# Transposing the attention weights of a prompt: from TensorE to 32x32 blocks on VectorE and a trip through DRAM

## The chip, the cores and the metric

The kernel runs on one core of a Trainium2 chip. A core has engines with an instruction list each, run in order: TensorE (PE in the profile; its weight loads are PEld), VectorE (DVE), ScalarE (ACT), GpSimd (POOL) and SyncE (SP). They meet by semaphores and through the on-chip memories SBUF and PSUM. DMAs to and from DRAM are issued here from the lists of SyncE and ScalarE; the profile shows these issues as SPq and ACTq, and the packets of the two as queues q1 (SyncE) and q10 (ScalarE). The metric is the time of one execution on the device in microseconds, and of several executions the median.

## The reference

One layer of a hybrid decoder. The prompt (1024 tokens, width 1024) and 8x4 sample tokens go through one input projection. Its columns feed an RWKV-7 time mixing (8 heads of 64) and a dilated attention: 3 groups of window and dilation, 4 heads of 128 each. Gates merge the two branches, an output projection and a LayerNorm follow. The change lies in the attention of the prompt:

```python
A_GROUPS = ((128, 1), (512, 4), (2048, 16))          # window, dilation
s = jnp.einsum('bdnqhe,bdnkhe->bdnhqk', qb, kc) * (1.0 / math.sqrt(E))
s = jnp.where(valid, s, NEG)
m = jnp.max(s, -1, keepdims=True)
p = jnp.exp(s - m)
l = jnp.sum(p, -1)
o = jnp.einsum('bdnhqk,bdnkhe->bdnqhe', p, vc)        # / l, then merged over the groups by softmax of the log sums
```

Tokens of one residue class modulo the dilation form a sequence, and each block of 128 queries sees its own block of keys and the one before. For 1024 tokens this makes, for a head, 8 query blocks in every group: with 15 blocks of 128x128 weights in group 0, 12 in group 1 and 8 in group 2, together 35 a head and 140 for four heads.

## The kernel before

**Stages.** Up to about 620 us the RWKV part runs. From there to about 1176 us come the projections of q, k and v for the 12 pairs of a head and a group, with the attention woven in; then two branches of the output stage and the LayerNorm.

**Projections.** A projection (`project_steps`) makes 128 columns for all tokens in three chunks of 352 tokens. Its weights arrive in two halves of 256 KB, by `load_w`: one DMA on SyncE (L159, `wraw`, 2 buffers), then a high part on ScalarE (L162, `whi`) and the rest on VectorE (L163, `wlo`), 3 buffers of each. A half feeds 36 matmuls on L172: 12 for each chunk, four each of high by high, high by low and low by high. ScalarE copies the finished chunk from PSUM (L820, `v`, `k` or `q`).

**Attention.** `attend` returns a list of steps for one head and group. They run among the 18 slots of 12 matmuls in which the next group's v, k and q are projected (`interleave`); a tile scheduler then fixes the order on each engine. The steps of the last group of a head also have the merge of the groups and the cached values of the sample tokens behind them, and the last group of all runs inside the output stage's first branch. The steps:

- `values`: VectorE transposes v in 32x32 blocks (L857); `values_out`: ScalarE issues four DMAs that put the blocks in place in DRAM (L863, `vs`); `values_in`: one DMA brings them back as `Vt`, tokens on partitions (L868).
- `scores`: for two or four query blocks TensorE makes scores into the one PSUM buffer `s` (L895). VectorE adds the mask and reduces the maximum (L897), negates it (L902, `nm`), and ScalarE takes the exponential in `Sm` with the row sum (L905).
- `old_keys` and `old_keys_out`: the same way for the keys that go out as a new cache (L875, four DMAs on L882).
- `turn`: up to four blocks of `Sm` are transposed on TensorE against the identity into PSUM (L915, tag `t`, 2 buffers) and copied to `PT` by ScalarE (L919) or VectorE (L921) in turn.
- `weigh`: four products of `Vt` and `PT` (L932), copied out to `o` on ScalarE (L937).

Turning the next four blocks and weighing the last four alternate, a slot or so apart. Between these steps stand those of the sample tokens: scores against cached keys on L1014 and L1033 with their reduce on L1022 and L1037, transposes of their weights on L1083, products with cached values on L1094; and `stats`, which transposes the sums of a group (L1133).

**DMA completion.** SyncE's and ScalarE's DMAs share eight semaphores for their completion, in turn; a DMA waits for the one eight places before it.

## Time and profile before

| | |
|---|---|
| median of 3 runs | 1381.0 us (1380.83 to 1381.04) |
| the profiled execution's own time | 1381.54 us |
| its span, first to last instruction | 1379.8 us |
| granted clock of TensorE | 0.996 |
| busy: PE, DVE, ACT, POOL | 97%, 58%, 34%, 5% |
| DMA packets | 340,270, of them 188,928 under 512 bytes |

A row of a group reads: line, engine, operation, tile written <- tiles read, partitions x elements, count; then busy time in all and nanoseconds of one; then the engine's idle time just before, with what ended it. A timeline row starts with the start time and the duration (of all in the row), in microseconds from the span's start. A row of a window has its length, then for each engine the busy time and in brackets the number of its instructions as the view counts them, then the granted clock, the DMA engines' busy share and GB/s. A row of waits has what waited, <- what released it, the total, the number of times and the longest. TensorE's timeline counts a product of two float32 blocks as two instructions, so x8 on L932 is four products; a transpose and a projection matmul count as one.

### The profile page before, as it was taken

How to read it: one execution, taken by the hardware profiler on the slowest of the kernel's cores; microseconds unless marked ns; L12 is line 12 of the kernel's file. 1: busy time of each engine (PE TensorE's matmuls, PEld its weight loads, DVE VectorE, ACT ScalarE, POOL GpSimd, SP SyncE). 2: the span in 40 equal slices, each digit the busy share in tenths (PEclk: the TensorE clock that was granted, in tenths of full speed). 3: DMA queues.
4: the chain of work that ended last, by engine and by line, in shares of the span. 5: the costliest groups of instructions: out<-in, count | busy, mean ns of one | idle time of the engine just before them, and what ended most of it. 6: DMA issues, size and time to landing. Idle time of an engine off the chain costs nothing.

```text
span 1379.8 us, 25342 instructions
## 1 busy us (share of the span) xinstructions
PE 1344.1 (97%) x9809; PEld 1245.0 (90%) x9809; DVE 804.0 (58%) x2203; ACT 467.2 (34%) x1089; POOL 67.2 (5%) x82
## 2 busy tenths in 40 slices
PE   7999999999999999999999999999999999899997
PEld 7998998898988889999999999999999998799786
DVE  4358767677867757441555275437542845665565
ACT  4333434444344444431332333233323234132211
POOL 0000000000000000000100000000000000015100
PEclk9999999999999999999999999999999999999999
DMA  6112222412322242336645355635554556795221
GB/s 216 55 47 73 58 82 72 110 37 75 88 59 75 74 110 79 91 94 123 136 106 132 84 141 115 131 93 140 114 123 115 133 122 153 230 287 170 82 103 68
DMA packets 340270, 151.62 MB, mean 110 GB/s; under 512 B 188928, under 2 KB 329622, under 8 KB 339894
## 3 DMA queue, kind: packets, MB, share of 16 engines
q1 hardware_dynamic: 241270, 129.68, 34.6%
q10 hardware_dynamic: 98880, 20.32, 7.4%
q8 instruction: 77, 1.26, 0.4%
q14 instruction: 43, 0.35, 0.1%
HBM read 110.68 MB, written 38.97 MB: 108 GB/s over the span
## 4 chain that ended last, share of the span: by engine, by line
PE 74%; DVE 14%; DMA 7%; issue 2%; ACT 2%; SPq 1%; DVEq 0%; ACTq 0%
PE pj L172 52%; PE pj L1378 7%; DVE tm L441 2%; DVE X L444 2%; PE o L932 2%; DMA cb<-cd 2%; PE s L895 2%; DMA wraw<-in_w_in_dram 1%; DVE wlo L163 1%; DVE o L1178 1%; PE t L915 1%; PE sc L503 1%; PE s L1014 1%; PE g L370 1%; DVE AT L377 1%
## 5 line engine op out<-in xcount | busy, mean ns | idle before, releaser
L172 PE MATMUL pj<-xhi,whi 128*128 128x352 f32 x1848 | 398.7, 337 | 5.0 <-ACT xhi L1245 3.0
L172 PE MATMUL pj<-xlo,whi 128*128 128x352 f32 x1848 | 382.8, 328 | 0.0
L172 PE MATMUL pj<-xhi,wlo 128*128 128x352 f32 x1848 | 381.9, 328 | 0.4 <-DVE wlo L163 0.4
L172 PEld LDWEIGHTS pj<-xhi,whi 128*128 128x128 f32 x1848 | 302.9, 189 | 21.7 <-issue 10.5
L172 PEld LDWEIGHTS pj<-xhi,wlo 128*128 128x128 f32 x1848 | 307.6, 189 | 3.6 <-issue 1.2
L172 PEld LDWEIGHTS pj<-xlo,whi 128*128 128x128 f32 x1848 | 307.9, 189 | 2.5 <-issue 0.4
L163 DVE TENSOR_TENSOR wlo<-wraw,whi 128x512 fp32r<-128x512 f32 x162 | 113.4, 701 | 84.0 <-ACT whi L162 83.3
L162 ACT ACTIVATE whi<-wraw 128x512 fp32r<-128x512 f32 x162 | 100.6, 625 | 146.6 <-PE pj L172 89.0
L905 ACT ACTIVATE Sm<-Sm,nm 128x128 f32<-128x128 f32 (+1 forms) x96 | 42.4, 442 | 102.7 <-DVE nm L902 102.7
L511 DVE SCALAR_TENSOR_TENSOR st<-sc,E,SD 64x64 f32<-64x64 f32 x128 | 36.2, 283 | 47.7 <-PE sc L508 46.2
L441 DVE TENSOR_TENSOR tm<-Y,X 128x60 f32<-128x60 f32 (+24 forms) x248 | 52.6, 212 | 6.3
L444 DVE TENSOR_TENSOR X<-X,tm 128x60 f32<-128x60 f32 (+24 forms) x248 | 52.0, 210 | 6.4
L1378 PE MATMUL pj<-wl,mh 128*128 128x512 f32 (+1 forms) x136 | 52.0, 382 | 0.0
L897 DVE CUSTOM_DVE_ANT_0 Sm<-s,cst 128x128 f32<-128x128 f32 (+1 forms) x96 | 29.2, 346 | 39.0 <-PE s L895 38.3
L494 ACT ACTIVATE SD<-st,E 128x128 f32<-128x128 f32 x64 | 25.6, 400 | 58.5 <-DVE st L511 58.5
L758 POOL TENSOR_TENSOR kvp<-vv,kv 128x512 f32<-128x512 f32 x16 | 19.7, 1233 | 514.3 <-DVE Ss L766 387.0
L932 PE MATMUL o<-PT,Vt 128*128 128x128 f32 x280 | 38.7, 276 | 0.8 <-ACT PT L919 0.8
L895 PE MATMUL s<-k,q 128*128 128x128 f32 (+1 forms) x192 | 37.8, 326 | 1.7 <-DVE ml L897 1.6
L820 ACT ACTIVATE k<-pj 128x352 f32<-128x352 f32 (+1 forms) x36 | 16.2, 454 | 67.5 <-PE pj L172 60.9
L932 PEld LDWEIGHTS o<-PT,Vt 128*128 128x128 f32 x280 | 36.4, 191 | 1.5 <-ACT PT L919 1.1
L503 PEld LDWEIGHTS sc<-R,AT 64*64 64x64 f32 x256 | 19.7, 134 | 18.4 <-DVE R L498 7.9
L299 ACT ACTIVATE zt<-pj,der 128x352 f32<-128x352 f32 x48 | 26.4, 551 | 27.9 <-PE pj L172 26.7
(314 smaller groups left out, 1719.1 us busy)
## 6 DMA issues: line engine op xcount, KB each, us to landing
wraw<-in_w_in_dram SPq DMA_DIRECT2D x146, 256.0 KB
gd<-zt SPq DMA_DIRECT2D x48, 176.0 KB
gt<-gd SPq DMA_DIRECT2D x48, 176.0 KB
vs<-bt ACTq DMA_DIRECT2D x48, 128.0 KB
kc<-in_cache_kv_g_dram SPq DMA_DIRECT2D x48, 128.0 KB
Vt<-vs ACTq DMA_DIRECT2D x12, 512.0 KB
cb<-cd SPq DMA_DIRECT2D x12, 512.0 KB
zd<-zt SPq DMA_DIRECT2D x24, 176.0 KB
```

Of the source, the lines that this page charges most:

```text
L162: S.activation(hi[:], raw[:], AF.Copy)
L163: V.tensor_tensor(lo[:], raw[:], hi.bitcast(F32)[:], ALU.subtract)
L172: T.matmul(out, w[wi][:, n % 4, :], x[:, n % 4, :], start=first and n == 0, stop=last and n == 11)
L441: V.tensor_tensor(tm, Y[:, r : r + 1, r + 1 : 32].to_broadcast([P, m, n]), X[:, 0:m, r : r + 1].to_broadcast([P, m, n]), ALU.mult)
L444: V.tensor_tensor(X[:, 0:m, r + 1 : 32], X[:, 0:m, r + 1 : 32], tm, ALU.subtract)
L503: T.matmul(pu[u, 64 * e : 64 * e + 64], AT[u, e, c, u], R[u, 64 * e : 64 * e + 64], start=True, stop=True)
L511: V.scalar_tensor_tensor(S1[d, d], pS[d, d], E[d, c, 64:65], SD[d, d], ALU.mult, ALU.add)
L895: T.matmul(r, qT[:, i * P : (i + 1) * P], kT[:, keys[i][0] * P : keys[i][0] * P + n], start=True, stop=True)
L897: V.tensor_tensor_reduce(out=Sm[:, i, 0:n], in0=r, in1=m3 if g == 2 else m12[:, 256 - n : 256], scale=1.0, scalar=NEG, op0=ALU.add, op1=AL ...
L905: S.activation(Sm[:, i, 0:n], Sm[:, i, 0:n], AF.Exp, scale=SCALE, bias=nm[:, x : x + 1], accum_out=ml[:, g, 1, i : i + 1])
L932: T.matmul(po[:, (i % 4) * P : (i % 4 + 1) * P], st["Vt"][:, kb_, :], PT[:, n * P : (n + 1) * P], start=m == 0, stop=m == len(keys[i]) - 1,)
L1378: T.matmul(pb[:], a[:, k], wk, start=x == 0, stop=x == len(prods) - 1)
```

## The change

`turn` no longer uses TensorE. The weights of a group are held in parts: two parts in groups 0 (7 and 8 blocks) and 1 (7 and 5), one of 8 in group 2, twenty in all, each an `Sm` tile of 128x1024 (2 buffers). When a part's exponentials are done, VectorE transposes it in 32x32 blocks (L918, `wt` in the tag `bt`, now 2 buffers), ScalarE issues four DMAs to DRAM, one for each band of 32 partitions (L926, `pt`, pieces of 128 bytes), and SyncE one DMA that brings the part back into the same `Sm` tile (L929). The products read `Sm` as their moving operand (now L939) and come last in the group's steps, in fours, just ahead of `stats`. The score buffer `s` has 2 PSUM buffers and `t` has 1. Behind the change the lines are seven or eight higher: L895, L897, L902, L905 become L903, L905, L910, L912; L1014, L1022, L1033 and L1037 become L1021, L1029, L1040 and L1044; L1083, L1094, L1133 become L1090, L1101, L1140.

```diff
-        return mk(pool, [parts, cols], tag, {"pj": PJ, "sc": 2, "g": 6 - PJ, "s": 1, "t": 2, "o": 1}[tag])
+        return mk(pool, [parts, cols], tag, {"pj": PJ, "sc": 2, "g": 6 - PJ, "s": 2, "t": 1, "o": 1}[tag])
...
+        parts = [[]]
+        for i, ks in enumerate(keys):
+            if len(parts[-1]) + 2 > 8 + (g == 2):
+                parts.append([])
+            parts[-1] += [(i, m, k) for m, k in enumerate(ks)]
...
         def turn(x):
-            part = pieces[x : x + 4]
-            b = ps("t")
-            for n, (i, m, _) in enumerate(part):
-                T.transpose(b[:, n * P : (n + 1) * P], st["Sm"][:, i, m * P : (m + 1) * P], ident)
-            PT = mk(ap, [P, 512], "PT", 2)
-            w = len(part) * P
-            if (x // 4) % 2:
-                S.activation(PT[:, 0:w], b[:, 0:w], AF.Copy)
-            else:
-                V.tensor_copy(PT[:, 0:w], b[:, 0:w])
-            st["PT", x] = PT
+            st["wt", x] = mk(ap, [P, SEQ], "bt", 2)
+            w = len(parts[x]) * P
+            V.transpose(st["wt", x][:, 0:w], st["Sm", x][:, 0:w])
+
+        def turn_out(x):
+            w = len(parts[x]) * P
+            d_ = st["wd", x] = mk(dpool, [P, w], f"pt{g}{h}{x}")
+            dv = d_.rearrange("(j t) (m q) -> t m j q", t=32, q=P)
+            for i in range(4):
+                rows = slice(32 * i, 32 * i + 32)
+                S.dma_start(dv[:, :, :, rows], st["wt", x][rows, 0:w].rearrange("t (m j q) -> t m j q", j=4, q=32))
+
+        def turn_in(x):
+            SP.dma_start(st["Sm", x][:, 0 : len(parts[x]) * P], st["wd", x][:])
...
-        steps += [values, sc[0], values_out, sc[1], values_in] + sc[2:] + [old_keys]
...
+        if g == 2:
+            steps += [values, sc[0], values_out, sc[1], values_in, x_(turn, 0), old_keys, x_(turn_out, 0)]
+            steps += [old_keys_out, x_(turn_in, 0)]
+        else:
+            steps += [values, sc[0], values_out, sc[1], values_in, sc[2], x_(turn, 0), sc[3], x_(turn_out, 0)]
+            steps += [x_(turn, 1), x_(turn_in, 0), x_(turn_out, 1), old_keys, x_(turn_in, 1), old_keys_out]
+        pieces = [p for part in parts for p in part]
+        return steps, [x_(weigh, pieces[x : x + 4]) for x in range(0, len(pieces), 4)]
...
-            k = 4 if g == 2 else 6
+            k = 5 if g == 2 else 8
...
-            steps += rest
+            steps += rest + w
```

How this moves the instructions is seen in group 2 of head 1. ScalarE's list there before; the x4 rows on L905 are the exponentials of four query blocks, whi_10419 is the weight half that the projection uses next, and whi_10515 the one after:

```order
L162 ACTIVATE whi_10419<-wraw_10417 128x512
L937 ACTIVATE o_10201<-o_10202 128x512
L882 DMA out_dram<-bt_10501 512x2x32
L820 ACTIVATE q_10276<-pj_10180 128x16x22
L882 DMA out_dram<-bt_10501 512x2x32
L820 ACTIVATE q_10276<-pj_10181 128x16x22
L937 ACTIVATE o_10201<-o_10247 128x512
L820 ACTIVATE q_10276<-pj_10182 128x16x20
L162 ACTIVATE whi_10515<-wraw_10513 128x512
...
L905 ACTIVATE Sm_10385,ml_8926<-Sm_10385,nm_10395 128x128 x4
```

Two weight halves are made ahead of the first exponentials. ScalarE's list at the same place after the change:

```order
L912 ACTIVATE Sm_10352,ml_8912<-Sm_10352,nm_10361 128x128 x4
L912 ACTIVATE Sm_10352,ml_8912<-Sm_10352,nm_10392 128x128 x4
L162 ACTIVATE whi_10400<-wraw_10398 128x512
L868 DMA Vt_10347<-vs_1881_10349 128x8x128
L926 DMA pt_1903_10499<-bt_10434 256x4x32
L820 ACTIVATE v_10416<-pj_10289 128x352
L820 ACTIVATE v_10416<-pj_10290 128x352
L926 DMA pt_1903_10499<-bt_10434 256x4x32
L820 ACTIVATE v_10416<-pj_10291 128x320
L162 ACTIVATE whi_10483<-wraw_10481 128x512
L926 DMA pt_1903_10499<-bt_10434 256x4x32 x2
L882 DMA out_dram<-bt_10469 512x2x32 x4
```

The weight half whi_10400 now stands behind all eight exponentials, the four writes are spread over the v copies, and whi_10483 stands behind the third v copy. TensorE's list at the same place after the change:

```order
L903 MATMUL s_10383<-k_10102,q_10276 128x128 x4
L1021 MATMUL s_10471<-KT_10453,qS_7764 32x64 x4
L1021 MATMUL s_10471<-KT_10476,qS_7764 32x64 x4
L1040 MATMUL s_10537<-kS_7765,qS_7764 32x4 x24
L172 MATMUL pj_10289<-xhi_8_86,whi_10400 128x352 x4
L172 MATMUL pj_10290<-xhi_8_86,whi_10400 128x352 x4
L172 MATMUL pj_10291<-xhi_8_86,whi_10400 128x352
L172 MATMUL pj_10289<-xhi_8_86,wlo_10401 128x352 x4
L172 MATMUL pj_10289<-xlo_10_88,whi_10400 128x352 x4
```

whi_10400 is needed after the second four scores and three rows of scores of the sample tokens, and the high-by-high matmuls of all three chunks are drawn ahead of the first that needs wlo_10401. Before, the twelve matmuls of a chunk stood together. SyncE's list in the stretch ahead of it:

```order
L929 DMA Sm_9904<-pt_1836_10038 128x896
L974 DMA kc_10726<-in_cache_kv_g_dram 128x4x128 x2
L159 DMA wraw_10292<-in_w_in_dram 128x4x128
L929 DMA Sm_9981<-pt_1851_10147 128x640
L159 DMA wraw_10398<-in_w_in_dram 128x4x128
```

Each read-back of a part of group 1 stands between the loads of the projection's weights.

More of the change, by code (lines that the diff above doesn't have):

```diff
@@ L882, in old_keys_out @@
                 S.dma_start(dst[:, :, :, rows], st["bt"][rows, 0:w].rearrange("t (c j x) -> t c j x", j=n, x=32))
+        parts = [[]]
[3 more added lines that the diff above has]
+            parts[-1] += [(i, m, k) for m, k in enumerate(ks)]
+        place = {(i, m): (x, n * P) for x, part in enumerate(parts) for n, (i, m, _) in enumerate(part)}
         def scores(blocks):
-            if blocks[0] == 0:
-                st["Sm"] = mk(ap, [P, 8, 256], "Sm", 1)
-            Sm = st["Sm"]
             b, off = ps("s"), 0
-            parts = []
+            rows = []
             for i in blocks:
                 n = P * len(keys[i])
-                parts.append((i, n, b[:, off : off + n]))
+                x, c = place[i, 0]
+                if c == 0:
+                    st["Sm", x] = mk(ap, [P, SEQ], "Sm", 2)
+                rows.append((i, n, b[:, off : off + n], st["Sm", x][:, c : c + n]))
                 off += n
-            for i, n, r in parts:
+            for i, n, r, _ in rows:
                 T.matmul(r, qT[:, i * P : (i + 1) * P], kT[:, keys[i][0] * P : keys[i][0] * P + n], start=True, stop=True)
-            for i, n, r in parts:
+            for i, n, r, Sm in rows:
                 V.tensor_tensor_reduce(
-                    out=Sm[:, i, 0:n], in0=r, in1=m3 if g == 2 else m12[:, 256 - n : 256], scale=1.0,
+                    out=Sm, in0=r, in1=m3 if g == 2 else m12[:, 256 - n : 256], scale=1.0,
                     scalar=NEG, op0=ALU.add, op1=ALU.max, accum_out=ml[:, g, 0, i : i + 1],
@@ L902, in scores, with weigh @@
             V.tensor_scalar(nm[:, 0 : len(blocks)], ml[:, g, 0, blocks[0] : blocks[-1] + 1], -SCALE, None, ALU.mult)
[L903 to L926 removed]
+            for x, (i, _, _, Sm) in enumerate(rows):
+                S.activation(Sm, Sm, AF.Exp, scale=SCALE, bias=nm[:, x : x + 1], accum_out=ml[:, g, 1, i : i + 1])
+        def turn(x):
+            st["wt", x] = mk(ap, [P, SEQ], "bt", 2)
[10 more added lines that the diff above has]
+            SP.dma_start(st["Sm", x][:, 0 : len(parts[x]) * P], st["wd", x][:])
+        def weigh(some):
+            for i, m, kb_ in some:
                 if m == 0 and i == 0:
@@ L931, in weigh @@
                 po, o = st["po"], os_[g]
+                x, c = place[i, m]
                 T.matmul(
[L933 removed]
+                    po[:, (i % 4) * P : (i % 4 + 1) * P], st["Vt"][:, kb_, :], st["Sm", x][:, c : c + P],
                     start=m == 0, stop=m == len(keys[i]) - 1,
@@ L937, in weigh, with seq @@
                     S.activation(o[:, (i // 4) * 512 : (i // 4 + 1) * 512], po[:], AF.Copy)
-        def both(f, g_):
-            return lambda: (f(), g_())
+        def seq(*fs):
+            return lambda: [f() for f in fs]
         n = 4 if g == 2 else 2
         sc = [(lambda i: lambda: scores(list(range(i, i + n))))(i) for i in range(0, 8, n)]
-        steps += [values, sc[0], values_out, sc[1], values_in] + sc[2:] + [old_keys]
-        xs = list(range(0, len(pieces), 4))
-        last = old_keys_out
-        for x in xs:
-            f = (lambda x: lambda: turn(x))(x)
-            steps.append(both(f, last) if x == 0 else both(last, f))
-            last = (lambda x: lambda: weigh(x))(x)
-        steps.append(last)
-        return steps
+        x_ = lambda f, x: lambda: f(x)
+        if g == 2:
[6 more added lines that the diff above has]
+        return steps, [x_(weigh, pieces[x : x + 4]) for x in range(0, len(pieces), 4)]
     smask = mk(sp, [P, 460], "smask")
```

16 lines of the change are left out of this document (3 added, 13 removed).

## The prediction

> **What bounds the kernel now.** I read the page first, for the engine that is never idle, then the windows over the attention stage, where all of the change lies.
>
> ```profile
> PE 1344.1 (97%) x9809; PEld 1245.0 (90%) x9809; DVE 804.0 (58%) x2203; ACT 467.2 (34%) x1089; POOL 67.2 (5%) x82
> 640.00:760.00 120.00, 119.59 (x771) 114.96 (x770) 57.03 (x134) 34.14 (x88) 7.10 (x6) 1.00 0.62 126
> 760.00:860.00 100.00, 99.29 (x741) 93.98 (x740) 54.31 (x125) 32.44 (x88) 3.90 (x3) 1.00 0.50 115
> 860.00:960.00 100.00, 99.87 (x739) 92.75 (x740) 54.87 (x129) 30.46 (x87) 3.63 (x3) 1.00 0.52 121
> 960.00:1060.00 100.00, 100.00 (x722) 94.72 (x721) 44.24 (x120) 32.50 (x86) 4.01 (x3) 1.00 0.49 106
> 1060.00:1180.00 120.00, 113.60 (x768) 105.47 (x767) 66.39 (x162) 39.71 (x103) 3.77 (x5) 0.99 0.63 147
> ```
>
> From 640 to 1060 us TensorE (PE) is busy for 418.75 of 420 us at full clock, VectorE (DVE) for half of it, ScalarE (ACT) for a third, the DMA engines for 0.49 to 0.62. So in this stage the time is the sum of TensorE's work, and a matmul taken away is gained in full, as long as everything that TensorE reads still arrives before its turn. How close that runs, the list of waits tells (total, times, longest):
>
> ```profile
> ACT whi L162 <- DMA wraw<-in_w_in_dram: 32.0, 11, 8.5
> ACT whi L162 <- DMA out_dram<-bt: 8.7, 1, 8.7
> PE s L895 <- DVE ml L897: 1.6, 2, 0.9
> SPq L159 <- DVE wlo L163: 136.8, 40, 8.0
> L172 PE MATMUL pj<-xhi,wlo 128*128 128x352 f32 x893 | 181.9, 325 | 0.4 <-DVE wlo L163 0.4
> ```
>
> ScalarE stands for up to 8.7 us in front of a weight tile, and yet the projections lost 0.4 us to it: three pairs of weight tiles are a cushion, each good for 36 matmuls, 5.8 us.
>
> **What the change removes.** One group of four transposes, in TensorE's timeline:
>
> ```profile
> 690.34 0.81 PE L172 MATMUL pj<-xlo,whi 128*128 128x352 f32 x4
> 690.99 0.60 PE L915 MATMUL t<-ident,Sm 128*128 128x128 f32 x4
> 691.34 0.89 PE L172 MATMUL pj<-xhi,whi 128*128 128x352 f32 x4
> L915 PE MATMUL t<-ident,Sm 128*128 128x128 f32 x140 | 21.9, 275 | 0.8 <-ACT Sm L905 0.7
> ```
>
> The four begin at 690.99 and the next work at 691.34, 0.35 us later, and its first four take 0.89 instead of 0.81: 0.43 us for a group. 140 transposes are 35 groups of four: **-15.1 us**. Their own busy time, 21.9, overlaps its neighbours and is the upper end. The second score buffer in PSUM should also end the two waits for L897, **-1.6 us** (0 if those waits were for something else).
>
> **What it adds, off TensorE.**
>
> ```profile
> L921 DVE COPY PT<-t 128x512 f32<-128x512 f32 x20 | 13.8, 689 | 19.4 <-PE t L915 19.4
> L919 ACT ACTIVATE PT<-t 128x512 f32<-128x512 f32 x12 | 7.2, 596 | 31.7 <-PE t L915 31.7
> L857 DVE STREAM_TRANSPOSE bt<-v 128x1024 f32<-128x1024 f32 x12 | 14.9, 1242 | 0.0
> 925.41 2.36 ACTq L882 DMA_DIRECT2D out_dram<-bt  x4
> ```
>
> VectorE loses 13.8 us of copies and gains 140 blocks at 1.242/8 = 0.155 us, 21.7: 8 us more over 540, under an engine that is half idle. ScalarE's copies (9.2 us with the four shorter ones) go, and 80 DMA issues come; L882 has the same kind of pattern and takes 2.36 us for four, 0.59 each, so 20 x 2.36 = 47 us of queue time in 540, where ACT is busy for 169. Both have room on average and I put both at nothing; if a weight tile is queued behind four issues just when it is due, the cost is up to 2.4 us a place.
>
> The transfers, from the packets of single microseconds (at 770 only 128-byte pieces move, at 742 512-byte ones) and from a value tile that is written and read back:
>
> ```profile
> q10 hardware_dynamic: 1102, 0.14, 97.3%
> q10 hardware_dynamic: 590, 0.30, 99.5%
> 917.45 0.31 ACTq L863 DMA_DIRECT2D vs<-bt  x1
> 919.73 0.38 ACTq L868 DMA_DIRECT2D Vt<-vs  x1
> 784.04 0.38 ACTq L868 DMA_DIRECT2D Vt<-vs  x1
> DMA  0000000000033322633235999999999996421100
> ```
>
> 140 blocks of 512 pieces are 71,680 packets, 65 us of all the DMA engines at 1102 a microsecond, spread over 540: the share rises by 0.12, to 0.6 or 0.75. One write of 1024 pieces has landed 2.28 us after its issue (917.45 to 919.73, where the read-back waits for it); a read-back of 512 KB, issued at 784.04, is done at 787.7 in the strip of 784 to 788, 3.7 us. A part therefore needs its transpose (1.24), four issues (2.36), the landing of the last (2.28 from its start) and 3.7 for coming back: 1.24 + 1.77 + 2.28 + 3.7 = 9.0 us after its last exponential if nothing stands between, against about 2 us for a TensorE transpose and copy. That is what putting the products last must hide.
>
> **Where TensorE now waits: group 2.** The program's order decides, as each engine runs its list in order. In heads 1 and 2 the weight tile whi that TensorE needs right after the second four scores and the cache scores stands on ScalarE behind all eight exponentials; before, it stood twelve rows ahead of them. The same chain in the trace of before, and what a whi takes:
>
> ```profile
> 897.73 1.05 PE L895 MATMUL s<-k,q 128*128 128x128 f32 x8
> 899.46 0.28 DVE L897 CUSTOM_DVE_ANT_0 Sm<-s,cst 128x128 f32<-128x128 f32 x1
> 900.48 0.40 ACT L905 ACTIVATE Sm<-Sm,nm 128x128 f32<-128x128 f32 x1 [1.56 <-DVE nm L902]
> 902.04 0.44 ACT L820 ACTIVATE v<-pj 128x352 f32<-128x352 f32 x1
> 902.55 0.32 PE L1014 MATMUL s<-KT,qS 128*32 128x64 f32 x8
> 911.03 0.98 PE L1033 MATMUL s<-kS,qS 128*32 128x4 f32 x48
> 919.71 0.62 ACT L162 ACTIVATE whi<-wraw 128x512 fp32r<-128x512 f32 x1
> ```
>
> Scores begin at 0 and last 0.9; two groups of cache scores at 0.25 and one at 0.9 follow, so TensorE wants the weights at 2.3. The last reduce ends at 2.0 (899.74), a cache reduce and the negation follow, the exponentials run from 2.7 to 4.2 (1.56 for four, 900.48 to 902.04), whi is there at 4.9: **2.6 us**. Then the third v copy and the next whi stand in one line behind the last of these 36 matmuls: 0.44 + 0.62, **1.1 us** more. The last two issues go out at 0.5 and 1.1 after those matmuls, the last write has landed at 3.4, the read-back at 7.1 plus a few tenths for the semaphores, and TensorE wants it at 1.1 + 5.8 = 6.9: **0.4 us**. That is 4.1 a head, 8.2 for two. In head 0 the whi stands between the two sets of exponentials, and the cache score comes later and covers 0.9: 0.8 and 0.4, 1.2. From below these waits are nothing, if the cushion reaches further than the order tells; from above each of three landings comes 4 us later in traffic, +12. I take 9.4, as each link has its row.
>
> **Groups 0 and 1.** Counted in the new order, at 1.95 us for twelve projection matmuls (three times the 0.65 from 690.34 to 690.99), their products come 17.8 to 24.6 us of TensorE work after their last scores, more than 9.0 plus the exponentials and the copies between. Only in heads 1 and 2 is the second part of group 0 short: its issues wait for the third k copy, and 0.5 + 2.36 + 1.7 + 3.7 and some tenths is 8.8 against 5.8 of projection, the stats, seven products and a slot, 8.5: 0.3 each, 0.6 (up to 3 each in traffic). Group 1 costs nothing. The last group of head 3 lies in the output stage, where TensorE waits anyway:
>
> ```profile
> 1176.42 0.95 PE L172 MATMUL pj<-xhi,whi 128*128 128x352 f32 x3 [3.03 <-ACT xhi L1245]
> ```
>
> That wait is for the branch's input, whose row of loads does not change; what the products add hides behind nine slots of projection. I put the tail at nothing (2 us either way).
>
> **The sum**: -15.1 - 1.6 + 9.4 + 0.6 = -6.7. The profiled execution took 1381.5 us (span 1379.8), half a microsecond over the median of 1381.0; from the median that is **1374 us**, and I give 1375, since the traffic leans only one way.
>
> **The rivals.** *All is hidden* (1364 to 1368): the new waits fall to the cushion and TensorE keeps 15 us. For it: waits of 8.7 us were absorbed before. Against it: an order in which whi comes after the exponentials it need not wait for. *The read-back only pays for itself* (1381): each of the twelve groups returns half a microsecond later than reckoned, 6 us. *Slower, by the weights* (1395): SyncE's queue, which loads the weights, now also issues the read-backs, and each waits there for its four writes to land, 1.77 + 2.28 = 4.1 us, with the next wraw queued behind it; DMAs of both queues also wait for an older one on their completion lane. A place where such a wait meets one of the 8.5 us that already stand uses up the cushion, and TensorE loses the 4.1. It decides from two places on; at five of the twenty parts it costs 20 us: 1375 + 20. For it: in the new order the high-by-high matmuls of another chunk are drawn ahead of the low ones at eleven places of the projections, so the low half was expected late there, and
>
> ```profile
> q1 hardware_dynamic: 45, 0.17, 50.5%
> q10 hardware_dynamic: 24, 0.00, 1.8%
> ```
>
> in the microsecond from 794, while large packets move on SyncE's queue, the small pieces of ScalarE's nearly stand (24 against 1102). Against it: SyncE already waits 136.8 us for low halves and TensorE lost nothing. [...]
>
> *Slower, by the pieces* (1393): the new writes put each 128-byte piece elsewhere in DRAM, and if such a piece costs twice the 1/1102 us, the four writes of a part need 7.4 us instead of 3.7. At the five short places (three in group 2, two in group 0) the products come 3.7 later, 18 us. Against it: the value tile is written in pieces of the same size, and landed after 2.28. [...]
>
> **Chances.** The forecast (waits in group 2 eat a third to nine tenths) 0.43, of which 0.11 lie within 0.2%; all hidden 0.16; pays for itself 0.08; slower by the weights 0.29, by the pieces 0.04. With 0.2%, 2.8 us, as what a measurement can tell: faster 0.48, within 0.19, slower 0.33. The forecast's own range is 1369 to 1382; the range that holds 8 in 10 runs from 1365, a little of the hidden case left out, to 1395, the price of the weights at five places.
>
> **What would show it.** No rows of L915; the five windows' TensorE time down by some 15 us; in group 2 of heads 1 and 2 TensorE's idle before a matmul with whi, released by ACT L162, 2 to 3 us; products (L939) released by a DMA into Sm by under 1 us. It is wrong if those gaps are missing (faster), or if gaps released by L162 or L163, with wraw late behind L929 on SyncE, stand in many places (slower).

## The result

| | before | after |
|---|---|---|
| median | 1380.96 us (1380.83 to 1381.04, 4 runs) | 1433.51 us (1431.35 to 1438.0, 4 runs) |
| span of the profiled execution | 1379.8 us | 1431.3 us |
| ratio | | 1.0392, 95% interval 1.0374 to 1.0409 |

The kernel is 52.6 us slower. The forecast was 1375, a little faster, with a range that ended at 1395. One timing of a later run, e9, took 2123.7 us at a granted clock of 0.56 and is left out of its median.

The page of the kernel after, first section (busy time of each engine, share of the span, instructions):

```profile
PE 1349.5 (94%) x9669; PEld 1251.4 (87%) x9669; DVE 810.4 (57%) x2203; ACT 457.9 (32%) x1073; POOL 67.1 (5%) x82
```

The 140 transposes are gone, 9809 - 9669, and yet TensorE is busy for longer, 1349.5 against 1344.1. Three terms make up the difference of the spans, 51.5 us. The idle time of TensorE grew from 1379.8 - 1344.1 = 35.7 to 1431.3 - 1349.5 = 81.8, by 46.1. The remaining matmuls, which should have taken 1344.1 - 15.1 = 1329.0 if the term of the prediction holds, took 20.5 more (e11 below has 1329.7 for the same 9669 instructions). And 15.1 went.

The windows of the kernel after (length, then for each engine the busy time and instructions, then granted clock, DMA share and GB/s), to set against those in the prediction:

```profile
640.00:760.00 120.00, 117.24 (x763) 112.44 (x762) 57.30 (x142) 31.64 (x86) 7.36 (x6) 1.00 0.68 136
760.00:860.00 100.00, 91.93 (x653) 86.96 (x652) 50.36 (x108) 27.87 (x76) 4.14 (x3) 0.95 0.69 154
860.00:960.00 100.00, 85.58 (x618) 79.90 (x617) 46.61 (x99) 25.33 (x70) 2.97 (x2) 0.93 0.61 143
960.00:1060.00 100.00, 95.45 (x657) 90.70 (x655) 51.30 (x135) 27.09 (x80) 5.07 (x4) 0.97 0.58 120
1060.00:1180.00 120.00, 106.55 (x690) 101.01 (x690) 59.94 (x136) 32.41 (x88) 2.58 (x2) 0.95 0.72 159
```

From 760 to 960 us TensorE now stands for 8 and 14 us in a stretch of 100 where it stood for less than one, and from 960 on for 5 and 13 us where it stood for 0 and 6. From 760 us on its clock is at 0.93 to 0.97 where it was at 0.99 to 1.00. What it waited for, in groups of its instructions from 620 to 1240 us (count, busy time, mean ns, idle time before and what ended it):

```profile
L172 PE MATMUL pj<-xhi,whi 128*128 128x352 f32 x913 | 204.8, 347 | 18.6 <-ACT whi L162 14.1 <-ACT xhi L1252 4.5
L172 PE MATMUL pj<-xhi,wlo 128*128 128x352 f32 x916 | 192.3, 333 | 1.3 <-DVE wlo L163 1.3
L939 PE MATMUL o<-Sm,Vt 128*128 128x128 f32 x269 | 39.0, 291 | 13.2 <-DMA Sm<-pt 13.2
L1101 PE MATMUL s<-kc,KT 128*32 128x128 f32 x72 | 3.9, 312 | 12.2 <-DVE KT L1092 12.1
```

So there are three waits of about equal size: for the projection's weights from ScalarE, for read-backs of the attention weights, and for `KT`, the attention weights of the sample tokens, which VectorE copies at L1092 by a line that the change did not touch.

Group 2 of head 1 is the place at which the prediction worked out its sum. TensorE's timeline there (start, duration, what, and the idle time before it with its cause):

```profile
910.64 1.72 PE L172 MATMUL pj<-xhi,whi 128*128 128x352 f32 x9 [1.51 <-ACT whi L162]
917.77 0.91 PE L172 MATMUL pj<-xhi,whi 128*128 128x352 f32 x4 [1.04 <-ACT whi L162]
926.97 1.16 PE L939 MATMUL o<-Sm,Vt 128*128 128x128 f32 x8 [3.04 <-DMA Sm<-pt]
945.03 0.66 PE L1101 MATMUL s<-kc,KT 128*32 128x128 f32 x8 [5.16 <-DVE KT L1092]
945.61 1.54 PE L172 MATMUL pj<-xhi,whi 128*128 128x352 f32 x4
```

The first two gaps are the two that were predicted, 1.5 and 1.0 us where 2.6 and 1.1 were forecast. The third is there too, but 3.0 instead of 0.4. The fourth was not forecast, and behind it four matmuls take 1.54 us instead of the 0.81 of the kernel before. The chain of waits over the same stretch says where the last two come from (start, duration, what):

```profile
916.85 0.58 ACTq L926
...
917.47 4.74 DMA pt<-bt
...
922.27 4.66 DMA Sm<-pt
...
928.16 0.46 ACT o L944
...
928.66 0.23 ACT nE L1164
...
930.06 3.87 DMA cd<-nE
...
934.34 6.08 DMA cb<-cd
...
940.45 1.98 DVE o L1185
...
944.51 0.47 DVE KT L1092
...
945.03 0.66 PE s L1101 x8
```

The last write of the part has landed at 922.21, 5.4 us after the start of its issue, where 2.28 was reckoned in the same way, and the read-back takes 4.7 instead of 3.7. Then one lateness makes the next: ScalarE copies out the late products (L944), and queued behind that copy is the exponential of the merge (L1164). With it the merge's coefficients make their own trip through DRAM, 10 us, VectorE's merge (L1185 and the lines behind it) waits for them, and behind the merge in VectorE's list stands the copy of `KT` for which TensorE then waits.

How full the DMA engines were meanwhile, in the eight microseconds from 915 (share of 40 slices in tenths; then each queue's packets, MB and share of the 16 engines):

```profile
DMA  9999998899999997799999999999999999999999
...
q1 hardware_dynamic: 2391, 1.05, 57.1%
q10 hardware_dynamic: 4815, 0.61, 50.4%
```

A mean share of 0.6 hid this: just where a part is on its way all engines are full, with the writes of the attention weights, their read-back, the old keys and the loads of the projection's weights in one place.

### The profile page after: what moved, and what is told of

Its sections match the earlier page's. It is cut to its first block, busy times and chain, and to the rows that moved or that the text cites. A ratio compares the mean times of both kernels' runs of the same rounds, so it can differ in the third digit from the quotient of the medians.

```text
span 1431.3 us, 25201 instructions
## 1 busy us (share of the span) xinstructions
PE 1349.5 (94%) x9669; PEld 1251.4 (87%) x9669; DVE 810.4 (57%) x2203; ACT 457.9 (32%) x1073; POOL 67.1 (5%) x82
## 3 DMA queue, kind: packets, MB, share of 16 engines
q10 hardware_dynamic: 171840, 29.50, 11.5%
## 4 chain that ended last, share of the span: by engine, by line
PE 72%; DVE 13%; DMA 10%; ACT 2%; issue 2%; ACTq 1%; SPq 0%; POOL 0%; DVEq 0%; POOLq 0%
PE pj L172 52%; PE pj L1385 6%; DMA Sm<-pt 2%; DVE tm L441 2%; DVE X L444 2%; PE o L939 2%; DMA pt<-bt 2%; PE s L903 2%; DMA cb<-cd 1%; PE sc L503 1%; DVE wlo L163 1%; DMA kc<-in_cache_kv_g_dram 1%; PE g L370 1%; DVE st L511 1%; PE sc L508 1%
## 5 line engine op out<-in xcount | busy, mean ns | idle before, releaser
L172 PE MATMUL pj<-xhi,whi 128*128 128x352 f32 x1848 | 403.1, 340 | 20.2 <-ACT whi L162 15.3
L172 PE MATMUL pj<-xhi,wlo 128*128 128x352 f32 x1848 | 387.5, 332 | 1.3 <-DVE wlo L163 1.3
L172 PE MATMUL pj<-xlo,whi 128*128 128x352 f32 x1848 | 387.1, 331 | 0.0
L172 PEld LDWEIGHTS pj<-xhi,whi 128*128 128x128 f32 x1848 | 310.0, 193 | 36.8 <-ACT whi L162 17.0
L172 PEld LDWEIGHTS pj<-xhi,wlo 128*128 128x128 f32 x1848 | 314.1, 193 | 5.1 <-DVE wlo L163 2.1
L172 PEld LDWEIGHTS pj<-xlo,whi 128*128 128x128 f32 x1848 | 313.4, 193 | 2.7 <-issue 0.6
L912 ACT ACTIVATE Sm<-Sm,nm 128x128 f32<-128x128 f32 (+1 forms) x96 | 42.3, 442 | 83.7 <-DVE nm L910 78.2
L905 DVE CUSTOM_DVE_ANT_0 Sm<-s,cst 128x128 f32<-128x128 f32 (+1 forms) x96 | 29.5, 348 | 63.5 <-PE s L903 63.5
L939 PE MATMUL o<-Sm,Vt 128*128 128x128 f32 x280 | 40.5, 291 | 13.4 <-DMA Sm<-pt 13.2
L939 PEld LDWEIGHTS o<-Sm,Vt 128*128 128x128 f32 x280 | 37.7, 203 | 16.1 <-DMA Sm<-pt 12.7
L820 ACT ACTIVATE q<-pj 128x352 f32<-128x352 f32 (+1 forms) x36 | 16.4, 456 | 66.7 <-PE pj L172 59.0
L903 PE MATMUL s<-k,q 128*128 128x128 f32 (+1 forms) x192 | 36.6, 322 | 0.0
```

Source lines behind the costliest of these rows:

```text
L172: T.matmul(out, w[wi][:, n % 4, :], x[:, n % 4, :], start=first and n == 0, stop=last and n == 11)
L820: S.activation(classes(dst[:], d)[:, :, t0 // d : (t0 + n) // d], b[:, 0:n].rearrange("p (i c) -> p c i", c=d), AF.Copy)
L903: T.matmul(r, qT[:, i * P : (i + 1) * P], kT[:, keys[i][0] * P : keys[i][0] * P + n], start=True, stop=True)
L905: V.tensor_tensor_reduce(out=Sm, in0=r, in1=m3 if g == 2 else m12[:, 256 - n : 256], scale=1.0, scalar=NEG, op0=ALU.add, op1=ALU.max, accu ...
L912: S.activation(Sm, Sm, AF.Exp, scale=SCALE, bias=nm[:, x : x + 1], accum_out=ml[:, g, 1, i : i + 1])
L939: T.matmul(po[:, (i % 4) * P : (i % 4 + 1) * P], st["Vt"][:, kb_, :], st["Sm", x][:, c : c + P], start=m == 0, stop=m == len(keys[i]) - 1,)
```

## The experiments

Five questions were open: whether the saving on TensorE is real, what the order and the steps cost without any trip, what the trip costs by its issues, its bytes or its pieces, what the products' waiting adds, and whether group 2 is the place. Each run was timed four to twelve times, beside runs of the kernel before on the same chip, whose medians lay between 1378.9 and 1380.7.

| run | median us | ratio to before, interval |
|---|---|---|
| the change | 1433.5 | 1.0392 (1.0374 to 1.0409) |
| e1 TensorE transposes, rest as changed | 1392.5 | 1.0102 (1.0083 to 1.0121) |
| e2 no trip, block transposes stay | 1392.8 | 1.0100 (1.0083 to 1.0118) |
| e3 whole trip, nothing waits for it | 1422.2 | 1.0301 (1.0273 to 1.0329) |
| e4 trip from GpSimd's list | 1419.4 | 1.0286 (1.0263 to 1.0310) |
| e5 as e3, a seventh of the bytes | 1400.5 | 1.0158 (1.0138 to 1.0179) |
| e6 as e3, whole rows, 20 writes | 1388.1 | 1.0061 (1.0041 to 1.0081) |
| e7 group 2 on TensorE | 1398.5 | 1.0134 (1.0114 to 1.0155) |
| e8 before, two score buffers | 1380.2 | 1.0008 (0.9996 to 1.0019) |
| e9 KT copied by ScalarE | 1432.7 | 1.0380 (1.0350 to 1.0410) |
| e10 no old keys from group 2 | 1422.4 | 1.0306 (1.0278 to 1.0334) |
| e11 before without its transposes | 1365.8 | 0.9894 (0.9877 to 0.9912) |
| e12 as e1, step numbers as before | 1399.2 | 1.0137 (1.0117 to 1.0156) |
| e13 as e2, products dealt out | 1390.9 | 1.0072 (1.0054 to 1.0090) |
| e14 as e2, cached values ahead of the merge | 1386.7 | 1.0048 (1.0033 to 1.0063) |
| e15 as e7, cached values ahead of the merge | 1413.4 | 1.0241 (1.0222 to 1.0259) |
| e16 as e2, no block transposes either | 1379.9 | 0.9999 (0.9981 to 1.0018) |
| e17 as e13, the old list of steps | 1376.2 | 0.9971 (0.9959 to 0.9983) |
| e18 as e11, the change's buffers | 1365.2 | 0.9889 (0.9869 to 0.9908) |

The scheduler lays out every one of these kernels anew, so a run differs from its neighbour by more than its edit, and no run shows what a new layout alone is worth: one edit of the order won 6 us on e2 and lost 15 on e7 (e14, e15). A difference of 8 to 15 us between two neighbours is therefore an indication; it stands better where a second pair of runs gives the same, and one of a few us is not read at all.

### First: the trip, the lists, the order

The first four runs were to tell whether the trip's lateness (A), the issues in ScalarE's and SyncE's lists (B) or the products' place (C) makes the loss.

```diff
 # e1
         def turn(x):
-            st["wt", x] = mk(ap, [P, SEQ], "bt", 2)
...
+            n = len(parts[x])
+            for a in range(0, n, 4):
+                b, w = ps("t"), min(4, n - a) * P
+                sm = st["Sm", x][:, a * P : a * P + w]
+                for m in range(0, w, P):
+                    T.transpose(b[:, m : m + P], sm[:, m : m + P], ident)
+                if a:
+                    S.activation(sm, b[:, 0:w], AF.Copy)
+                else:
+                    V.tensor_copy(sm, b[:, 0:w])
...                                                    # turn_out and turn_in: pass
 # e2
         def turn_out(x):
-            ...
+            pass
         def turn_in(x):
-            ...
+            pass
 # e3
-            SP.dma_start(st["Sm", x][:, 0 : len(parts[x]) * P], st["wd", x][:])
+            SP.dma_start(mk(dpool, [P, len(parts[x]) * P], f"sink{g}{h}{x}")[:], st["wd", x][:])
 # e4
-                S.dma_start(dv[:, :, :, rows], st["wt", x][rows, 0:w]....)
+                G.dma_start(dv[:, :, :, rows], st["wt", x][rows, 0:w]....)
-            SP.dma_start(st["Sm", x][:, 0 : len(parts[x]) * P], st["wd", x][:])
+            G.dma_start(st["Sm", x][:, 0 : len(parts[x]) * P], st["wd", x][:])
```

> The changed kernel with only the route of the transposes put back: each part of the weights is transposed on TensorE (140 transposes, into the single PSUM buffer t) and copied back into the same Sm tile; the eighty writes and twenty read-backs are gone, the products still come last in a group. Theory A (the loss of 52.5 us is the trip itself: late read-backs, what is queued behind them, and a TensorE clock that falls when it stands): near the kernel before, 1378 to 1388, and granted clock 0.99 again. Rival B (the 100 extra DMA issues block ScalarE's and SyncE's lists in front of the weights, whether or not a product waits for them): the same, 1378 to 1388. Rival C (products last is the cause: the merge of the groups starts later and VectorE's copies for the cached values queue behind it, the 12 us before L1101): 1395 or more, with that wait still there.

> The changed kernel without the eighty writes and twenty read-backs: VectorE still transposes the parts in blocks, but the products take the weights as they are, untransposed; left out is thus the placing of the transposed blocks. Same products, same number of TensorE instructions as the changed kernel, no trip to wait for. Theory A: the saving of the prediction appears, 1364 to 1369. Rival B: the same. Rival C: the products are still last, so the wait before L1101 stays and the time is above 1381.

> The changed kernel with all hundred DMAs issued from the same lists, but each read-back goes to a place in DRAM that nothing reads, and the products take the untransposed weights at once; left out is the use of the transposed blocks. The traffic and the issues stay, the products wait for no DMA. Theory A in its narrow form (products waiting for their read-back start everything): at most 1385. Rival B (issues, completion lanes and traffic hold up weights and the merge): 1410 to 1430, with TensorE waiting for whi as before.

> The changed kernel with writes and read-backs issued from GpSimd's list, which is busy 5% of the time, in place of ScalarE's and SyncE's. Complete computation. Theory A: the trip is as long or longer, so 1425 to 1450. Rival B: the two lists are free again, so most of the loss goes, 1375 to 1400.

Measured: 1392.5, 1392.8, 1422.2 and 1419.4. None of the three theories has it alone, and e1 and e4 lie in none of their ranges. With no trip at all, e2 lies 13 us over the kernel before instead of 15 under it: 28 us come from what is left of the change, and C's bound held in e2, though not its reason (below). From e2 to e3, where nothing waits for the trip, it is 29 us more, so B's range held and A in its narrow form is out. From e3 to the change, where the products wait, 11 more. Waits from 620 to 1240 us in e3, three of ScalarE and one of TensorE (total, times, longest):

```profile
ACT whi L162 <- DMA out_dram<-bt: 24.4, 6, 7.0
ACT Sa L1052 <- DMA out_dram<-bt: 24.1, 3, 13.2
ACT whi L162 <- DMA pt<-bt: 12.8, 3, 5.4
PE pj L172 <- ACT whi L162: 22.6, 16, 4.6
```

ScalarE stands in front of a weight tile or a softmax until an earlier DMA of small pieces has landed. Neither instruction touches what these DMAs read or write; so the wait is put down to the DMA issues ahead of the instruction in ScalarE's list, which wait for the older DMA on their completion lane. In the trace of the kernel after the 823 DMAs of SyncE and the 212 of ScalarE share eight semaphores, and each but the first eight was issued behind a wait, in its own list, for the semaphore that it then used. TensorE in turn waits 22.6 us for weight tiles, where it waits 1.9 in e2. Before, one wait of ScalarE's of this kind is there, 8.7 us. In e4 these lists are free of the trip, but the time falls by 14 us only. VectorE's timeline in e4 has what is in the way, and a row of TensorE's waits the price:

```profile
768.85 0.68 DVE L163 TENSOR_TENSOR wlo<-wraw,whi 128x512 fp32r<-128x512 f32 x1
778.09 1.25 DVE L857 STREAM_TRANSPOSE bt<-v 128x1024 f32<-128x1024 f32 x1 [8.56 <-DMA pt<-bt]
...
PE pj L172 <- DVE wlo L163: 22.3, 6, 6.0
```

The next value tile is transposed into a buffer `bt` that the writes of the weights still hold, for 8.6 us, and the low halves of the weights are queued behind it. So the buffer is shared by three users with one slow reader, and moving the issue to another list moves the wait to VectorE. The run changes more than the list: DMAs from GpSimd's list show up on a queue of their own (q0, software), where a write of 128 KB lands 6.2 us after its issue in the median.

### Issues, bytes or pieces; group 2; the score buffer

```diff
 # e5: the first block of a part alone
-                S.dma_start(dv[:, :, :, rows], st["wt", x][rows, 0:w]....)
+                S.dma_start(dv[:, 0:1, :, rows], st["wt", x][rows, 0:P]....)
-            SP.dma_start(sink[...], st["wd", x][:])
+            SP.dma_start(sink[...], st["wd", x][:, 0:P])
 # e6: one write of a part, in whole rows
-            for i in range(4):
-                S.dma_start(dv[:, :, :, rows], st["wt", x][rows, 0:w]....)
+            S.dma_start(d_[:], st["wt", x][:, 0:w])
 # e7: turn as in e1 for group 2, no trip there
 # e8, on the kernel before
-"s": 1, "t": 2, "o": 1}
+"s": 2, "t": 1, "o": 1}
```

> The run with the read-backs to an unread place in DRAM (1422 us), but each of the eighty writes and twenty read-backs carries only the first block of its part; left out as there is the use of the transposed blocks, and seven eighths of the bytes. Issues and completion lanes are unchanged. Theory B1 (the number of issues and the lane and landing waits in ScalarE's and SyncE's lists are the cost): 1410 to 1422, ScalarE's whi still waiting for landings. Theory B2 (the traffic, 65 us of small packets, makes everything land late): 1392 to 1400, close to the run without a trip.

> The run with the read-backs to an unread place, but each part is written by one DMA in rows of 2.5 to 4 KB in place of four DMAs in 128-byte pieces: all bytes, 20 write issues in place of 80; left out is the crossing of the blocks and the use of the transposed blocks. B1 (issues): 1395 to 1402, most of the 29 us between 1393 and 1422 gone. B2 (bytes): above 1405. B3 (the pieces, not the bytes): near 1400 too, and then the run with few bytes must fall as well.

> The changed kernel, complete, with group 2 alone put back to TensorE transposes (32 of 140; parts of groups 0 and 1 still go through DRAM): 16 of 20 parts make the trip. The prediction's reading (the short covers of group 2 are where it hurts): 1395 to 1405. If the issues count wherever they stand: 1433 less a fifth of 41 for the trip, plus 3.5 for the transposes, 1425 to 1430.

> The kernel before with one edit, the score buffer s in two PSUM buffers and t in one. By the prediction's term (two waits for L897 end) 1.6 us less, 1377 to 1380. If the single t buffer makes the alternating transposes wait for the copies: 1383 to 1395, and then this edit is a part of the loss of the run with TensorE transposes and products last (1392).

Measured: 1400.5, 1388.1, 1398.5 and, over twelve timings, 1380.2. The run e6 moves all bytes of e3 and is 34 us faster, below all three of its ranges; e5 issues every DMA of e3 and is 22 us faster. So it is not the bytes (B2), and issues that carry little cost at most the 8 us from e2 to e5 (B1). What e5 and e6 both take away are most of the 71,680 pieces of 128 bytes: B3. Not told apart is how far the pieces need the eighty issues to do their harm, since e6 has twenty; twenty issues of 128-byte pieces were not run. The same bytes in rows of 2.5 to 4 KB cost nothing that can be told from e2 (1388.1 against 1392.8 us).

Two waits of e6, over the same stretch as above:

```profile
ACT whi L162 <- DMA wraw<-in_w_in_dram: 17.8, 9, 3.4
DVE bt L857 <- DMA pt<-bt: 12.1, 10, 3.0
```

On ScalarE nothing waits for a landing of `pt` or of the old keys any more; on VectorE the value tiles still do. TensorE's wait for weight tiles is 7.6 us (e3 22.6, e5 5.4).

e7 shows the place. Four parts of twenty less make the trip, 32 transposes return to TensorE (3.5 us by the prediction's term), and the time falls by 35 us, two thirds of the loss. No product waits for a read-back any more, in groups 0 and 1 either, and what is left is 6 us over e1, which has no trip at all. That group 2 is where the trip hurts was right. That it hurts there by its short covers is not shown: e3, where no product needs a cover, already has 29 of the 41 us that the trip costs. e8 changes nothing (0.9996 to 1.0019): the two waits for L897 are gone from its trace, and the term of -1.6 us is still not there, though 1.6 us, 0.1%, is also about half the width of that interval.

### Where the lateness goes; the price of the transposes

```diff
 # e9
-            if s_:          # the second KT: VectorE, the first: ScalarE
+            if False:       # both ScalarE
 # e10: old_keys_out
+            if g == 2 and h:
+                return
 # e11, on the kernel before: turn empty, products read Sm
-                    ... st["Vt"][:, kb_, :], PT[:, n * P : (n + 1) * P],
+                    ... st["Vt"][:, kb_, :], st["Sm"][:, i, m * P : (m + 1) * P],
 # e12, on e1
-            k = 5 if g == 2 else 8
+            k = 4 if g == 2 else 6
```

> The changed kernel, complete, with one edit: the copies of the second half of the cached weights KT, on VectorE at L1092 behind the merge, go to ScalarE like the first half. If the 12 us before L1101 and the slower clock behind those waits come from VectorE's list alone: 1412 to 1421. If the products' lateness only shows elsewhere next (the loads of cached values, the next weights): 1428 to 1436.

> The changed kernel without the four DMAs that write the old keys of group 2 in heads 1 to 3 (L882, left out there); they come right behind the four writes of the weights in ScalarE's list, in pieces of 128 bytes too. If pieces that pile up on ScalarE's queue in group 2 are the cause: 1405 to 1420, with the landing of the last write of a part, 4.7 us now, nearer 3. If the weights' own 4096 pieces suffice: 1428 to 1436.

> The kernel before, in its own interleaving, with its 140 transposes and their copies left out: the products take the weights untransposed. The price of the term that the whole change was for. By the prediction's term, -15.1: 1363 to 1367. If TensorE's time there is not the bound after all (as the run without a trip, 1393, might have it): above 1372.

> The run with TensorE transposes and products last (1392), with the number of steps ahead of the first cached score put back (k = 6 and 4 in place of 8 and 5). If the later start of the cached scores makes the 12 us: 1380 to 1384. If the products' place makes them: 1389 to 1395, with the waits for kc still there.

Measured: 1432.7, 1422.4, 1365.8 and 1399.2. In e9 the wait for the KT copy is gone and another has taken its place. TensorE's timeline there:

```profile
801.23 0.66 PE L1101 MATMUL s<-kc,KT 128*32 128x128 f32 x8 [4.78 <-DMA kc<-in_cache_kv_g_dram]
950.47 0.43 PE L1101 MATMUL s<-kc,KT 128*32 128x128 f32 x8 [4.11 <-DMA kc<-in_cache_kv_g_dram]
```

The cached values now come as late as KT did. VectorE's list was therefore only the last link; a lateness that comes from further up was not taken away at the end of its chain (1432.7 us against 1433.5). Leaving the old keys out (e10) wins 11 us, between its two ranges, and in head 1 the last write of a part has landed 3.2 us after the start of its issue instead of 5.4. So other small pieces on ScalarE's queue seem to have a share, but the weights' own do most of it.

e11 is the price of the term on which the change rests: 1.06% or 14.0 us of the kernel before (interval 0.88 to 1.23%) for 140 transposes and their copies together, where 15.1 was worked out for the transposes from three rows of a timeline and the copies were put at nothing. TensorE's busy time falls by 14.4 (1344.1 to 1329.7). This term was right.

e12 lies in neither of its ranges, 7 us over e1 in place of 10 under it: the step numbers alone are not it.

### What came with the route

Left was that e2, without trip and transposes on TensorE, is 27 us over e11.

```diff
 # e13, on e2: products dealt out among the cached scores
-            rest = a[k:]
+            rest, w = a[k:] + w, []
 # e14, on e2, and e15, on e7
-  steps += [me[0], sv[1], me[1], sv[2], sv[3], me[2], sv[4], me[3], sv[5], sv[6], me[4], me[5], sv[7]]
+  steps += [me[0], sv[1], sv[2], sv[3], sv[4], sv[5], me[1], sv[6], me[2], me[3], me[4], me[5], sv[7]]
 # e16, on e2: turn empty
 # e17, on e13: the steps of the kernel before, k = 4 and 6, turn in one step with the first products
 # e18, on e11
-"s": 1, "t": 2, "o": 1}
+"s": 2, "t": 1, "o": 1}
-            st["bt"] = mk(ap, [P, SEQ], "bt", 1)
+            st["bt"] = mk(ap, [P, SEQ], "bt", 2)
```

> The run without a trip (1393), with one edit in the order of the steps: the products, in fours, are dealt out among the cached scores as in the kernel before, in place of last. Parts, step numbers, buffers and everything else as there; untransposed weights as there. If the products' place is what costs 27 us between 1366 (the kernel before without its transposes) and 1393: 1364 to 1372. If it is the other edits (two score buffers, the step numbers, the moved old keys): 1386 to 1396.

> The run without a trip (1393), with the products with cached values dealt out ahead of the loads for the merge, so that their loads (kc, L974) stand ahead of the merge's (cb, L1180) in SyncE's list; left out is what was left out there. If kc behind cb is what the later products cost: the 12.6 us of waits for kc and the slow clock behind them go, 1374 to 1382. If the waits move on to the merge: 1388 to 1396.

> The complete kernel with group 2 on TensorE and groups 0 and 1 through DRAM (1398), with the same edit: products with cached values ahead of the merge's loads. If that edit helps as hoped: 1380 to 1390. Otherwise 1394 to 1402.

> The run without a trip (1393) without VectorE's twenty block transposes as well (left out: the whole transposing). If VectorE's 22 us of transposes, which stand in its list ahead of low halves and reduces, are the cost: 1366 to 1374. If it is the order or the buffers: 1386 to 1393.

> The run with the products dealt out and without a trip (1391), with the list of steps as in the kernel before: old keys after the scores, no steps of their own for transposes and trip (the block transposes are issued with the first products), k = 4 and 6. If the count and order of the steps, which set how far the merge and the cached values have come when the next group's scores arrive, is the cost: 1364 to 1372. If the buffers or the block transposes are: 1386 to 1393.

> The kernel before without its transposes (1366) with the change's buffers: s in two PSUM buffers, t in one, bt in two. If the single t buffer, which the weights of the cached values, the stats and the new keys still use, costs what the order does not: 1380 to 1393. Otherwise 1362 to 1368.

Measured: 1390.9, 1386.7, 1413.4, 1379.9, 1376.2 and 1365.2; of e16 and e17 there are ten timings each. The buffers cost nothing (e18). The products' place as such costs next to nothing (e13 against e2), which ends theory C in the form in which it stood. e14, e16 and e17 lie between their two ranges, e15 over both; for e16 and e17 the reason is that neither edit is the whole. Two things remain, and between them they make the sum: the twenty block transposes on VectorE (e2 to e16, 13 us; by the other pair, e17 to e18, 11) and the new list of steps (e13 to e17, 15 us; e16 to e18, 15). 1390.9 - 13 - 15 is 1363, and e18 has 1365. A check from another side is e1, with the new list and TensorE's transposes: e16's 1379.9 and the 14.0 of e11 make 1393.9, and e1 has 1392.5. e1 and e2 are equal, so the block transposes alone, without any trip, cost as much as the transposes on TensorE. e14 turned the loads round and won 6 us, and the same edit on e7 lost 15, so it decides nothing.

In e2, e16 and e17 TensorE waits most for a load that the change did not touch. Its row from 620 to 1240 us in the kernel before, e2, e16 and e17:

```profile
PE s L1094 <- DMA kc<-in_cache_kv_g_dram: 2.1, 2, 1.2
...
PE s L1096 <- DMA kc<-in_cache_kv_g_dram: 12.6, 5, 4.3
...
PE s L1094 <- DMA kc<-in_cache_kv_g_dram: 12.2, 5, 3.5
...
PE s L1093 <- DMA kc<-in_cache_kv_g_dram: 10.0, 5, 2.8
```

The products with cached values stand for their loads (`kc`) for 10 to 12.6 us in e2, e13, e16 and e17, which have the new list, the block transposes or both, and for under one in e11 and e18. Either edit alone brings this wait, so it does not explain why the two costs add; and why the loads come late is not shown.

How the block transposes take their 13 us, by the pages of e2 and e16:

```profile
PE 1337.4 (96%) x9669; PEld 1237.5 (89%) x9669; DVE 809.5 (58%) x2203; ACT 457.9 (33%) x1073; POOL 69.1 (5%) x82
```

```profile
PE 1327.2 (96%) x9669; PEld 1233.3 (90%) x9669; DVE 790.4 (57%) x2183; ACT 458.9 (33%) x1073; POOL 66.3 (5%) x82
```

TensorE has the same instructions in both, and 10.2 of the 13.4 us between the spans (1389.3 and 1375.9) are the same matmuls running longer; only 3.2 are idle time. The granted clock stood at half for 38 us in e2 and for 28 in e16, which is a part of it. By what chain twenty transposes of VectorE, 19 us in an engine busy for 58%, bring more slow stretches, is not shown. Nor is which step of the new list costs the 15 us. No kernel that computes the whole beat the kernel before.

## The prediction, point by point

**TensorE's saving (-15.1): right.** e11 measured 14.0, with the copies. The way to it (what a group of four displaces in the timeline, not its busy time of 21.9) holds.

**The score buffer (-1.6): not there.** e8 is 1.0008. The two waits for L897 went, as forecast, and the time did not fall with them.

**Waits in group 2 (+9.4): right in place and links, too small.** In heads 1 and 2 the first two gaps were 1.5 and 1.0 us (2.6 and 1.1 forecast), the third 3.0 and 2.1 (0.4). In head 0 they were 2.0 before the weights and 1.3 before the products (0.8 and 0.4). Together that is 13.4 us, and the sizes of the single gaps were off both ways. The step that failed in it is the time of the trip: "the landing of the last (2.28 from its start) and 3.7 for coming back" came from a lone write and a lone read-back. With the pieces of three users in one place they took 5.4 and 4.7 in head 1, 4.1 us more together. The tail, put at nothing, has waits for weights of 2.2 and 3.4 us at 1137 and 1211 us.

**Groups 0 and 1 (+0.6): wrong in group 1.** "Group 1 costs nothing", but two of its products waited 2.4 and 2.6 us. The chain there, for head 1:

```profile
876.13 0.72 DVE KT L1010
...
876.87 0.37 SPq L970
...
877.42 4.71 DMA Sm<-pt
...
882.17 1.86 PE o L939 x7
```

The read-back stands in SyncE's list behind a load of cached values (L970), which waits until VectorE is done with L1010. The prediction counted the cover from the writes' landing, and not the queue past which the read-back had been put.

**Costs at nothing off TensorE: this is the step that lost most.** "Both have room on average and I put both at nothing." VectorE was reckoned at 8 us more, the block transposes less the copies. The twenty block transposes alone cost 11 to 13 us of the time (e16, e17), as much as the transposes and copies that they replaced, and the writes in ScalarE's list with their traffic cost 29 (e3 less e2) before any product waited. An average share of a stage was used for engines that run a list in order: at 0.6 mean DMA share the engines were full for eight microseconds on end just when a part was under way, and ScalarE stood for up to 13 us.

**The order of the steps: not in the sum at all.** The prediction read the new order at three places, and had no term for the list of steps as a whole. e13 and e17 put it at 15 us, e18 and e16 too.

**The clock: not in the sum.** Every wait was priced at its own length. 20.5 of the 51.5 us are matmuls that ran longer. By windows of half a microsecond the granted clock stood at half for 74 us of the kernel after and for 14 of the one before, and TensorE was busy in 57 and 7 of them; at half clock four projection matmuls took 1.54 us in place of 0.81, and half of the 50 more is an estimated 25 us, so the clock is enough for all of it.

**The rivals.** Slower by the weights (1395, 0.29) and by the pieces (1393, 0.04) came nearest, and both were right in name and wrong in mechanism. Waits from 620 to 1240 us of the kernel after, and queue q10 of the whole run, before and after:

```profile
SPq L929 <- DMA pt<-bt: 31.2, 13, 7.6
ACT whi L162 <- DMA wraw<-in_w_in_dram: 23.6, 10, 3.9
ACT whi L162 <- DMA out_dram<-bt: 30.7, 6, 6.9
...
q10 hardware_dynamic: 98880, 20.32, 7.4%
...
q10 hardware_dynamic: 171840, 29.50, 11.5%
```

The read-backs did wait on SyncE for their writes, 31.2 us in all, as the first rival says. But `whi` waited less for its raw half than before, 23.6 us in place of 32.0; what it waited for more were landings ahead of it in ScalarE's own list, 30.7 us of old keys alone where it was 8.7. The second rival needs a piece to cost twice as much. The pieces that the change adds took 11.5% of 1431.3 less 7.4% of 1379.8, some 62 us, where 65 was reckoned: their own time was right, and what they held up in other lists (e3 to e6, 34 us) was not in the price. What made the second rival's chance small was a row that did not fit the case, "the value tile is written in pieces of the same size, and landed after 2.28": one tile at a time, with nothing beside it.

By the runs, in the order in which they lead from the kernel before to the change: -14 for the transposes and copies (e11), 0 for the buffers (e18), +15 for the list of steps with the products' place (e18 to e16), +13 for VectorE's block transposes (e16 to e2), +29 for the trip that nothing waits for (e3), of which some 8 for issues that carry little and 22 for the rest of the pieces (e5), and +11 for the products that wait (the change). That is +54, against 52.6 measured. Each step is the difference of two neighbours, so that the sum comes out is no proof of its terms; of them only the first, the 15 and the 13 have a second pair of runs or a check.

## What to carry to other kernels

A transfer is to be priced in the traffic of the microseconds in which it runs, with all that shares its queue, its buffer and its completion lanes there; a lone transfer and a mean share over the stage were both lower ends here (2.28 us to the landing of a lone write, 5.4 for the last write of a part; a mean DMA share of 0.6, and all engines full for eight microseconds). Pieces of 128 bytes made the distance large: e3, with 71,680 of them, took 34 us more than e6, which moves the same bytes in whole rows by twenty writes. Where an engine that is 97% busy is fed by lists that run in order, taking work from it and giving it to those lists can lose several times the gain, here 52.6 us in all where 14.0 were gained, because one late DMA held up everything behind it: ScalarE stood for up to 13.2 us at a time (e3), VectorE for 8.6 (e4) and TensorE for 5.2 (the change). Work moved off the busiest engine was not free on one that is busy for 58%: twenty block transposes on VectorE cost 11 to 13 us, and the 140 on TensorE with their copies 14.0. A wait on TensorE cost its length here and, in each of the ten windows of 3.41 us that waits left with less than 1.5 us of its work, 3.4 to 10.2 us at half clock besides.

## What the runs showed of the hardware

The clock behind a wait. Windows of the kernel after (length, then for each engine the busy time and instructions; the column before the last two is the granted clock):

```profile
765.39:768.80 3.41, 1.46 (x52) 1.36 (x52) 1.08 (x6) 1.07 (x2) 0.00 (x0) 1.00 1.12 245
768.80:772.21 3.41, 3.41 (x13) 3.40 (x12) 0.75 (x4) 0.00 (x0) 0.00 (x0) 0.50 0.82 158
...
922.40:925.81 3.41, 1.53 (x10) 1.24 (x8) 2.14 (x4) 1.95 (x5) 0.00 (x0) 1.00 0.95 195
925.81:929.22 3.41, 2.25 (x18) 2.26 (x19) 0.63 (x3) 1.06 (x4) 0.00 (x0) 1.00 0.70 154
```

Between 620 and 1300 us the granted clock of this kernel fell to half twelve times and came back twelve times. Read from windows of half a microsecond, all 24 changes lie on one grid of 3.41 us, wherever the waits began. Ten windows of this grid at full clock had TensorE busy for less than 1.5 us, for 0.20 to 1.46 and so in none idle throughout, and behind each the clock was at 0.50, for 3.4 to 10.2 us. Of six windows with 1.5 to 2.0 us busy, two were followed by half the clock and four were not. So a wait of 1.95 us (ended at 768.34) brought the half clock, and one of 3.04 us (ended at 926.97), which lies across two windows, did not.
